# A hybrid attention and DeltaNet trunk: attention filled into the chunk scan by proportion, scores tied behind the scan's matmuls, output weights loaded from step 7

## The chip, the cores and the metric

The kernel runs on one core of a Trainium2 chip. The metric is the device time of one execution in microseconds (us); lower is better. The kernel before takes 2121.76 us, the median of three runs (2119.16 to 2123.61). The profiled execution took 2120.93 us. The engines are named as the profile names them: PE (TensorE matmuls), PEld (its weight loads), DVE (VectorE), ACT (ScalarE), POOL (GpSimd), SP (SyncE, which here only issues transfers).

## The reference, cut to what matters

Two layers run over 256 context tokens and 512 latent tokens of width 1024. In each layer one input projection feeds two kinds of heads that share one output projection; a mixture of experts follows.

```python
# softmax attention: 8 query heads, 2 key heads
s = einsum("bqkgd,bskd->bkgqs", q, k) * ATTN_SCALE
a = einsum("bkgqs,bskd->bqkgd", softmax(s), v)          # context rows attend in layer 0 only
# gated DeltaNet: 8 heads, chunks of 64 tokens, forward and backward
def step(state, xs):                                     # 12 chunks in order, one after another
    v_new = u_i - w_i @ state
    o_i   = qd_i @ state + a_i @ v_new
    state = state * exp(gl_i) + kd_i.T @ v_new
x = x + gate * (concat(a, norm(o) * silu(g)) @ w_out)    # output projection
x = x + gate2 * moe(modulate(norm(x)))                   # 32 experts, top 2
```

The modulation vectors (gates, shifts, scales) of the layer come from `silu(c) @ ada_w`, a matrix of 1024 by 6144 per layer. Attention and the scan need nothing of each other; the output projection needs both.

## The kernel before, in words

Every tile has 128 partitions. Matmul operands are split into a high and a low part, so a product takes three matmuls (`mm3`), and a score takes two (`attn_scores`, against the key stacks `ka` and `kb`).

The change lies in the part of `layer` that runs the scan and the attention together. It is run once per layer. Three streams are written as Python generators:

- **The scan**, `delta_step`, d: 12 steps, both directions at once. A step has four TensorE parts with VectorE or ScalarE work between them: `ks` (keys against the state; left out in step 0), `pz` (the chunk's corrected values, after DVE's `yt` and `lk`), `su` (the state's update, after DVE's `w`), then `po` and `pq` (the chunk's output, `pq` against the state; later added up by DVE in `ot` and by POOL in `o`). The generator yields eight times, after each TensorE part and after each part beside it.
- **The attention**, `attn_slots`, f: a unit is one query tile of one head. Four calls bring it on by scores (`sc`, into one PSUM buffer of two banks), maximum (DVE, `pp`), exponential and scale (ACT), transposes (`ptr`), high and low parts (`ph` by ACT, `pl` by DVE), values (`pv`) and output (`fu`, stored to `atd`). Layer 0 has 16 units of context and 32 of latent rows, layer 1 the 32.
- **The modulation**, `ada_steps`, a: `ada_w` is read in pieces of 1 MB (`araw`, two buffers, issued on POOL's queue) and multiplied (`aps`): 24 pieces in layer 0, 16 in layer 1.

In the kernel before, a string per step (`PAT`, three per layer, used in turn) says in which order the streams are called: one letter, one call. `step_load` brings the next step's chunk (`lk`, `lx`, `lq`) on SP's queue, and POOL multiplies `lq` into `lx`. From step 4 (`WS`) the first three quarters of `w_out` (`wr`, 1 MB each) are loaded on SP's queue too. Behind the loop they are split (`woh`, then `wol`, `m` or `wr` for the low parts), the fourth quarter is loaded into the first one's buffer, and the output projection (`po` of line 240) begins. Its tiles read the attention back (`al<-atd`) and turn the scan's output (`ot` of line 1048). Gates and shifts (`g`, `m`, `s`, with `h` for a norm's weight) come by broadcasting loads, which reuse the attention's memory.

The order in which the generators are called is not the order on the engines. A scheduler orders each engine's instructions by a simulation of its own; the calls give priorities, and a manual dependency without a semaphore (`add_manual_dep` with NoSync, or `issue_after`) fixes the order of two instructions of one engine. Each engine then runs strictly in that order: an instruction that waits holds up all that stand behind it on its engine or queue.

## Time and profile before

| | before |
|---|---|
| time, median of 3 runs | 2121.76 us |
| the profiled execution, its time and span | 2120.93 us, 2119.0 us |
| PE busy | 1768.4 us (83%) |
| DVE busy | 1459.2 us (69%) |
| ACT busy | 1019.6 us (48%) |
| POOL busy | 854.5 us (40%) |
| mean granted TensorE clock | 0.889 of full speed |
| loop of layer 0, first `pz` to last `pq` | 393.3 to 619.5 us |
| loop of layer 1, first `pz` to last `pq` | 1487.6 to 1655.9 us |

Busy time is an average over stages, so the profile is read by stretches. A stretch's length less PE's busy time is PE's idle time. The granted clock has two levels, 1.2 and 2.4 GHz; a value between them is a mean over the stretch, with 1.00 for 2.4 GHz. A wait stands in brackets behind the instruction that it delayed, with what ended it. The waits of an engine that is not late for anybody cost nothing.

### The profile page before, as it was taken

How to read it: one execution, taken by the hardware profiler on the slowest of the kernel's cores; microseconds unless marked ns; L12 is line 12 of the kernel's file. 1: busy time of each engine (PE TensorE's matmuls, PEld its weight loads, DVE VectorE, ACT ScalarE, POOL GpSimd, SP SyncE). 2: the span in 40 equal slices, each digit the busy share in tenths (PEclk: the TensorE clock that was granted, in tenths of full speed). 3: DMA queues.
4: the chain of work that ended last, by engine and by line, in shares of the span. 5: the costliest groups of instructions: out<-in, count | busy, mean ns of one | idle time of the engine just before them, and what ended most of it. 6: DMA issues, size and time to landing. Idle time of an engine off the chain costs nothing. (4 is left out here: it accounts for less than half of the span.)

```text
span 2119.0 us, 35656 instructions
## 1 busy us (share of the span) xinstructions
PE 1768.4 (83%) x13835; PEld 1388.6 (66%) x13835; DVE 1459.2 (69%) x2552; ACT 1019.6 (48%) x1595; POOL 854.5 (40%) x915
## 2 busy tenths in 40 slices
PE   6998898778976859998995987876898587999994
PEld 4887777655655747766764866765676475777773
DVE  4469996457772468987875579992587455787774
ACT  4444345445641136665554544333576224666663
POOL 4455653144354423233324466651233453334231
PEclk9998797679997979999997998975899698999997
DMA  8222436767655489998864223435983548988872
GB/s 279 78 82 77 119 112 176 232 191 212 209 135 124 116 310 334 331 333 322 312 223 122 75 73 93 137 108 162 273 241 104 143 179 326 344 335 327 334 296 98
DMA packets 227686, 427.80 MB, mean 202 GB/s; under 512 B 83720, under 2 KB 157180, under 8 KB 202939
## 3 DMA queue, kind: packets, MB, share of 16 engines
q1 hardware_dynamic: 171547, 329.09, 46.6%
q0 software_dynamic: 33536, 72.59, 12.0%
q10 hardware_dynamic: 22432, 23.81, 3.3%
q8 instruction: 110, 1.80, 0.4%
q14 instruction: 61, 0.50, 0.1%
HBM read 386.82 MB, written 84.67 MB: 223 GB/s over the span
## 5 line engine op out<-in xcount | busy, mean ns | idle before, releaser
L1421 POOL DMA_INDIRECT yd<-ey,idx x64 | 110.4, 1725 | 427.6 <-DMA yd<-ey,idx 120.8
L1367 PE MATMUL pab<-w,xt 128*128 128x512 f32 x512 | 230.3, 592 | 0.0
L1335 ACT ACTIVATE w2h<-w 128x2048 fp32r<-128x2048 f32 x64 | 122.7, 1917 | 130.9 <-PE py L1409 83.9
L1336 DVE TENSOR_TENSOR w2l<-w,w2h 128x2048 fp32r<-128x2048 f32 x64 | 147.8, 2309 | 45.8 <-ACT w2h L1335 45.8
L1336 DVE TENSOR_TENSOR w13l<-w,w13h 128x2048 fp32r<-128x2048 f32 x64 | 146.4, 2288 | 29.3 <-ACT w13h L1335 29.3
L1367 PEld LDWEIGHTS pab<-w,xt 128*128 128x128 f32 x512 | 93.0, 191 | 92.0 <-issue 91.8
L490 POOL TENSOR_TENSOR wlo<-wraw,whi 128x1024 fp32r<-128x1024 f32 (+1 forms) x44 | 113.6, 2586 | 92.5 <-ACT whi L489 92.5
L240 PE MATMUL pn<-whi,hh 128*128 128x256 f32 (+1 forms) x432 | 137.0, 320 | 12.9 <-ACT gev L1565 8.0
L240 PE MATMUL pn<-whi,hl 128*128 128x256 f32 (+1 forms) x432 | 135.7, 317 | 1.8 <-DVE hl L351 1.6
L240 PE MATMUL pn<-wlo,hh 128*128 128x256 f32 (+1 forms) x432 | 134.0, 311 | 1.2 <-POOL wlo L490 1.2
L240 PE MATMUL po<-woh,m 128*128 128x512 f32 x320 | 108.9, 419 | 24.6 <-ACT woh L1072 16.9
L1335 ACT ACTIVATE w13h<-w 128x2048 fp32r<-128x2048 f32 x64 | 121.7, 1902 | 6.3 <-DMA w<-w 3.9
L240 PE MATMUL pt<-hh,wlo 128*128 128x512 f32 (+1 forms) x352 | 123.5, 351 | 0.0
L240 PE MATMUL pt<-hh,whi 128*128 128x512 f32 (+1 forms) x352 | 122.1, 347 | 0.0
L240 PE MATMUL pt<-hl,whi 128*128 128x512 f32 (+1 forms) x352 | 121.5, 345 | 0.0
L1409 PE MATMUL py<-w2h,gh 128*128 128x512 f32 x256 | 108.8, 425 | 5.5 <-DVE ey L1416 4.4
L1416 DVE TENSOR_TENSOR ey<-py,eg 128x1024 f32<-128x1024 f32 x64 | 78.2, 1223 | 48.5 <-PE py L1409 36.2
L1340 POOL DMA_INDIRECT xe<-h2d,idx x64 | 87.0, 1359 | 60.8 <-issue 24.3
L519 DVE SCALAR_TENSOR_TENSOR dT<-xin,cw,dT 128x772 f32<-128x772 f32 x64 | 80.1, 1252 | 43.3 <-ACT dT L517 41.5
L1409 PE MATMUL py<-w2h,gl 128*128 128x512 f32 x256 | 102.7, 401 | 5.0 <-DVE gl L1388 5.0
L240 PEld LDWEIGHTS pn<-whi,hh 128*128 128x128 f32 x432 | 92.2, 214 | 19.3 <-ACT gev L1565 9.1
L1351 PEld LDWEIGHTS xt<-cst,xe 128*128 128x128 f32 x512 | 68.4, 192 | 55.3 <-issue 29.8
(402 smaller groups left out, 5130.4 us busy)
## 6 DMA issues: line engine op xcount, KB each, us to landing
w<-w SPq DMA_DIRECT2D x192, 1024.0 KB
araw<-ada_w POOLq DMA_DIRECT2D x40, 1024.0 KB, 8.6
wraw<-w_in SPq DMA_DIRECT2D x40, 512.0 KB
lk<-vk SPq DMA_DIRECT2D x48, 256.0 KB
lx<-xad SPq DMA_DIRECT2D x40, 256.0 KB
araw<-ada_w SPq DMA_DIRECT2D x8, 1024.0 KB
wr<-w_out SPq DMA_DIRECT2D x8, 1024.0 KB
vk<-vr ACTq DMA_DIRECT2D x16, 384.0 KB
```

Source lines behind the costliest of these rows:

```text
L240: self.nc.tensor.matmul(ps, a(k), b(k), start=(first and n == 0), stop=(last and n == 3 * nk - 1))
L490: getattr(nc, eng).tensor_tensor(lo, raw, hi, op=OP.subtract)
L519: nc.vector.scalar_tensor_tensor(dst, xin[:, tap:tap + 772], cw[:, tap, f:f + 1], dst, op0=OP.mult, op1=OP.add)
L1335: self.pin(nc.scalar.activation(hi, src, AF.Copy))
L1336: self.pin(nc.vector.tensor_tensor(lo, src, hi, op=OP.subtract))
L1340: self.pin(self.nc.gpsimd.indirect_dma_start(out=xe, out_offset=None, in_=h2d, in_offset=bass.IndirectOffsetOnAxis(ap=idx, axis=0), bounds ...
L1351: pin(nc.tensor.transpose(ps[:, k * P:(k + 1) * P], xe.rearrange("p (q k) -> p k q", k=8)[:, 4 * q + k, :], self.ident))
L1367: self.pin(self.nc.tensor.matmul(out, xt[:, k, :], w13[:, :, KS + k, :], start=False, stop=(k == 3)))
L1409: pin(self.nc.tensor.matmul(py[:, n * 512:(n + 1) * 512], a[:, j, :], b[:, c], start=(j + m == 0), stop=(j == 1 and m == 2)))
L1416: pin(nc.vector.tensor_tensor(y, py, gates, op=OP.mult))
L1421: self.pin(self.nc.gpsimd.indirect_dma_start(out=yd, out_offset=bass.IndirectOffsetOnAxis(ap=idx, axis=0), in_=y, in_offset=None, bounds_c ...
```

## The change

The strings `PAT` go. Behind each TensorE part of a step (every second yield) `advance` calls the attention and the modulation until both have had their share: all calls spread evenly over 11.5 of the 12 steps (`FS`), less the calls made ahead (`PRE`, 32 in layer 0, that is 8 units, and none in layer 1). Every score matmul is ordered behind the last matmul of the scan that was written in front of it (`step_mm`). The three loads of `w_out` are written from step 7 on instead of 4, one per step, and are ordered on SP's queue behind the load of `lx` that was written last (`stepx`).

```diff
-WS = 4
-PAT = (('fdfdfffdfffafddffffdfaffdfd', ...
+WS = 7
+PRE, FS = (32, 0), 11.5
...
     def attn_scores(self, u, st):
-                self.pin(self.nc.tensor.matmul(u.ps[:, a:b], qt, st[n][:, u.h // 4, a:b], start=(n == 0), stop=(n == 1)))
+                m = self.nc.tensor.matmul(u.ps[:, a:b], qt, st[n][:, u.h // 4, a:b], start=(n == 0), stop=(n == 1))
+                if self.step_mm is not None:
+                    self.tc.add_manual_dep(m.ins, self.step_mm, mybir.DependencyInfo(mybir.DependencyClass.NoSync, mybir.DependencyReason.DATA), reason="order")
...
     def step_load(...):
-            self.q("step").dma_start(x[rows[d], :np_], xad[tl[d], d, rows[d], :np_])
+            self.stepx = self.q("step").dma_start(x[rows[d], :np_], xad[tl[d], d, rows[d], :np_])
...
     def delta_step(...):        # so for ks, pq, pz, su and po
-                        pin(nc.tensor.matmul(ps[e][rows[d], ...
+                        self.step_mm = nc.tensor.matmul(ps[e][rows[d], ...).ins.name
...
     def layer(...):
             fill = self.attn_slots(work, st, qd, atd, pool)
+            total = dict(f=4 * (sum(2 * nq for _, _, nq, _ in work) + 2), a=4 * (4 if last else 6))
+            given = dict(f=0, a=0)
+            for _ in range(PRE[i]):
+                next(fill)
+                given["f"] += 1
+            ahead_f = PRE[i]
+
+            def advance(part):
+
+                for nm, gen, z in (("f", fill, ahead_f), ("a", ada, 0)):
+                    while given[nm] < z + part * (total[nm] - z):
+                        next(gen, None)
+                        given[nm] += 1
+
...
                 for s in range(12):
                     nkx = load(s + 1)
-                    step = self.delta_step(s, S, kx, dT, sc, o, seen, need(D0[s] // 2), p2)
-                    for c in PAT[i][s % 3]:
-                        next({"d": step, "f": fill, "a": ada}[c], None)
+                    for j, _ in enumerate(self.delta_step(s, S, kx, dT, sc, o, seen, need(D0[s] // 2), p2)):
+                        if j % 2 == 0:
+                            advance((4 * s + j // 2 + 1) / (4 * FS))
                     kx = nkx
                     if s >= WS and len(raws) < WP:
-                        raws.append(self.wout_raw(i, len(raws), wrp.tile([P, 2 * D], F32, name="wr", tag="wr%d" % len(raws))))
+                        with tc.issue_after(self.stepx.ins):
+                            raws.append(self.wout_raw(i, len(raws), wrp.tile([P, 2 * D], F32, name="wr", tag="wr%d" % len(raws))))
+                self.step_mm = None
```

Lines behind the edits move by 2 (helpers) to 18 (end of `layer`), so the same instruction has another line number in the rows of the change. No instruction is added or taken away: PE, DVE, ACT, POOL and SP have as many as before. The order is the same up to the end of layer 0's convolutions and in both expert stages.

SP's queue in layer 0's loop, before, where the first `w_out` loads stand (`lq`, `lk`, `lx`: the chunk of a step; `wr`: a quarter of `w_out`):

```order
L868 DMA lx<-xad_89 64x1024
L872 DMA lq<-qkd_90 64x512 x4
L1065 DMA wr<-w_out 128x2x1024 x3
L872 DMA lq<-qkd_90 64x512 x2
L867 DMA lk<-vk_88 64x1024 x2
L868 DMA lx<-xad_89 64x1024 x2
```

The same queue in the change, near the loop's end:

```order
L870 DMA lx<-xad_89 64x1024 x2
L1067 DMA wr<-w_out 128x2x1024
L874 DMA lq<-qkd_90 64x512 x2
L869 DMA lk<-vk_88 64x1024 x2
L870 DMA lx<-xad_89 64x1024 x2
L1067 DMA wr<-w_out 128x2x1024
L874 DMA lq<-qkd_90 64x512 x2
```

The three loads stood in one piece behind the chunks of the first two steps; they now stand one by one behind the chunks of steps 8, 9 and 10. In layer 1 they move in the same way. The fourth quarter moves forward a little: in layer 0 it stands behind the two gate loads `g` of line 1703 and two of the small `mm` loads, and in the change directly behind the four `m3t` loads; in layer 1 it stands behind two loads `al`, and in the change in front of them.

PE in layer 1, step 10 (one before the last), between values and state update, before:

```order
L648 MATMUL pv<-ph,vs 128x512
L648 MATMUL pv<-pl,vs 128x512
L920 MATMUL pz<-lk,lx 64x64 x16
L935 MATMUL su_16353<-w,lk 64x64
L935 MATMUL su_16354<-w,lk 64x64
```

The same place in the change:

```order
L605 MATMUL sc<-ka,qs 128x256
L605 MATMUL sc<-kb,qs 128x256
L266 MATMUL aps<-araw,scp 32x256 x8
L631 MATMUL ptr<-cst,pp 128x128 x6
L922 MATMUL pz<-lk,lx 64x64 x16
L605 MATMUL sc<-ka,qs 128x512
L605 MATMUL sc<-kb,qs 128x512
L605 MATMUL sc<-ka,qs 128x256
L605 MATMUL sc<-kb,qs 128x256
L937 MATMUL su_16411<-w,lk 64x64
L937 MATMUL su_16412<-w,lk 64x64
```

Before, the last values of the attention stand in front of this `pz`, and steps 10 and 11 have nothing beside them. In the change transposes and modulation stand in front of the `ks` of step 11 too, and the attention's last values between that `ks` and the last `pz` (in layer 0 behind the last `pz`).

DVE behind layer 1's loop, before (`yt`, `lk`: step 11; `s<-s,h`: a scale table for after the projection; `ot`: output of step 11; `m`, `wol`: operands of the output projection):

```order
L912 TENSOR_TENSOR yt_16496<-ks_16463,scs 128x4x64
L912 TENSOR_TENSOR yt_16496<-ks_16464,scs 128x4x64
L913 TENSOR_TENSOR lk<-lk,yt_16496 128x512
L1717 SCALAR_TENSOR_TENSOR s_16721<-s_16721,h_16792 128x1024
L959 TENSOR_TENSOR ot<-pq_16564,scs 128x4x64
L959 TENSOR_TENSOR ot<-pq_16565,scs 128x4x64
L960 TENSOR_TENSOR ot<-ot,po 128x512
L1051 TENSOR_TENSOR m_16592<-ot,m_16592 128x512
L1051 TENSOR_TENSOR m_16593<-ot,m_16592 128x512
L1073 TENSOR_TENSOR wol<-wr,woh 128x1024
```

The same place in the change:

```order
L962 TENSOR_TENSOR ot<-ot,po 128x512
L1053 TENSOR_TENSOR m_16623<-ot,m_16623 128x512
L1053 TENSOR_TENSOR m_16624<-ot,m_16623 128x512
L1075 TENSOR_TENSOR wol<-wr,woh 128x1024 x2
L1075 TENSOR_TENSOR m_16624<-wr,woh 128x1024
L1075 TENSOR_TENSOR wr<-wr,woh 128x1024
L1028 TENSOR_REDUCE oss<-o_16815 128x8
L1030 TENSOR_TENSOR oss<-oss,fq 128x8
L1031 TENSOR_TENSOR oss<-oss,fq 128x8
L1032 TENSOR_SCALAR oss<-oss 128x8
L1028 TENSOR_REDUCE oss<-o_16909 128x8
L1735 SCALAR_TENSOR_TENSOR s_16721<-s_16721,h_16792 128x1024
```

The scale table stood in front of the last output of the scan; it now stands behind it and behind the first four low parts of `w_out` that DVE makes. On ACT the six first `woh` stand in front of the second `m<-al` in layer 1 instead of behind it. In layer 0 the two last `wr<-wr,woh` of DVE stand in front of `sw<-mm,nmw` (line 308) instead of behind it.

## Rows read from the trace of the kernel before

**Rows 1.** Busy time by stretches: stretch, length, PE, PEld, DVE, ACT, POOL, clock, DMA, GB/s.

```profile
349.60:393.30 43.70, 37.98 (x363) 31.53 (x362) 20.34 (x69) 31.09 (x78) 3.35 (x5) 0.50 0.52 151
393.30:454.90 61.60, 37.99 (x523) 26.83 (x522) 24.95 (x66) 21.46 (x50) 19.07 (x23) 0.69 0.83 247
454.90:619.50 164.60, 139.03 (x2151) 106.60 (x2150) 120.43 (x279) 94.59 (x176) 69.38 (x75) 0.95 0.65 187
619.50:671.30 51.80, 27.35 (x102) 21.12 (x102) 23.58 (x28) 12.01 (x16) 20.45 (x13) 0.74 0.57 131
...
1487.60:1534.50 46.90, 39.76 (x497) 29.55 (x496) 28.44 (x67) 26.09 (x49) 11.47 (x14) 0.84 0.95 279
1534.50:1635.80 101.30, 93.77 (x1504) 72.90 (x1502) 84.51 (x194) 70.48 (x132) 33.20 (x38) 1.00 0.63 184
1635.80:1655.90 20.10, 10.74 (x257) 9.90 (x256) 8.88 (x22) 3.04 (x5) 13.06 (x13) 0.66 0.47 129
1655.90:1701.20 45.30, 24.62 (x101) 20.44 (x101) 21.41 (x27) 11.71 (x15) 19.76 (x12) 0.70 0.45 116
```

**Rows 2.** PE's waits from 393 to 455 us: total, times, longest.

```profile
PE aps L266 <- DMA araw<-ada_w: 16.6, 2, 13.7
PE sc L605 <- DVE qs L595: 5.3, 1, 5.3
```

**Rows 3.** Timeline of SP's queue, layer 0: start, duration, instruction.

```profile
398.16 1.61 SPq L1065 DMA_DIRECT2D wr<-w_out  x3
...
407.89 2.42 SPq L868 DMA_DIRECT2D lx<-xad  x2
```

**Rows 4.** Timeline of POOL, layer 0.

```profile
427.38 1.28 POOL L873 TENSOR_TENSOR lx<-lx,lq 128x512 f32<-128x512 f32 x1 [16.19 <-DMA lx<-xad]
...
440.97 0.74 POOL L232 DMA_DIRECT2D araw<-ada_w  x1
```

**Rows 5.** The tile `araw`: time from issue to landing.

```profile
DMA to landing us min/median/max: 5.2/8.6/16.8
```

**Rows 6.** PE's waits from 455 to 619.5 us.

```profile
PE aps L266 <- DMA araw<-ada_w: 9.0, 4, 3.8
```

**Rows 7.** Timeline of SP's queue, layer 1.

```profile
1493.39 1.10 SPq L1065 DMA_DIRECT2D wr<-w_out  x2
```

**Rows 8.** Timeline of PE, layer 1, early in the loop.

```profile
1515.21 1.30 PE L266 MATMUL aps<-araw,scp 128*32 128x256 f32 x16 [2.17 <-DMA araw<-ada_w]
1523.54 1.94 PE L266 MATMUL aps<-araw,scp 128*32 128x256 f32 x16 [3.61 <-DMA araw<-ada_w]
```

**Rows 9.** Timeline of PE, layer 1, the last steps and behind the loop.

```profile
1641.79 1.14 PE L935 MATMUL su<-w,lk 64*64 64x64 f32 x32 [4.82 <-DVE w L924]
...
1670.96 1.94 PE L1048 MATMUL ot<-cst,o 128*128 128x128 f32 x8 [15.10 <-DVE ot L959]
...
1681.78 1.65 PE L240 MATMUL po<-woh,m 128*128 128x512 f32 x3 [5.62 <-ACT woh L1072]
```

**Rows 10.** Timeline of DVE and ACT, behind layer 1's loop.

```profile
1669.25 1.23 DVE L1717 SCALAR_TENSOR_TENSOR s<-s,h 128x1024 f32<-128x1024 f32 x1 [19.15 <-DMA h<-norm_ffn_w]
...
1680.15 0.63 ACT L1044 ACTIVATE m<-al 128x512 fp32r<-128x512 f32 x1 [6.62 <-DMA al<-atd]
```

**Rows 11.** Timeline of PE, behind layer 0's loop.

```profile
657.52 1.22 PE L240 MATMUL po<-woh,m 128*128 128x512 f32 x2 [9.57 <-ACT woh L1072]
...
665.22 0.80 PE L240 MATMUL po<-wr,m 128*128 128x512 f32 x1 [5.30 <-DVE wr L1073]
```

**Rows 12.** Timeline of SP's queue, behind layer 0's loop.

```profile
630.76 7.73 SPq L1109 DMA_DIRECT2D m3t<-md  x4
...
644.57 0.89 SPq L1065 DMA_DIRECT2D wr<-w_out  x1
```

**Rows 13.** Timeline of ACT and DVE, behind layer 0's loop.

```profile
656.41 2.00 ACT L1072 ACTIVATE woh<-wr 128x1024 fp32r<-128x1024 f32 x2 [24.53 <-DMA wr<-w_out]
...
662.62 1.40 DVE L308 SCALAR_TENSOR_TENSOR sw<-mm,nmw 128x8 f32<-128x8 f32 x2 [16.32 <-DMA nmw<-norm_mix_w]
```

More of the change, by code (lines that the diff above doesn't have):

```diff
@@ L128 @@
 WP = 3
-WS = 4
-PAT = (('fdfdfffdfffafddffffdfaffdfd', 'fdfffdffdfdfafddffdfafffdfaf', 'fdffdfffdfdfafddffdfafffdff'), ('fdffdffadffdfddafdffdf', 'fdffdffadffdfddafdffdf', 'fdffdffddadffdfadd'))
+WS = 7
+PRE, FS = (32, 0), 11.5
 WB = 2
@@ L158, in __init__ @@
         self.pins(False)
-        self.seq = None
+        self.seq = self.step_mm = None
         self.mh = self.cp.tile([P, 32], F32, name="mh")
@@ L900, in by_state @@
                         r = slice(64 * e, 64 * e + 64)
-                        pin(nc.tensor.matmul(ps[e][rows[d], pr * HD:(pr + 1) * HD], dT[j][r, pr, col[d]:col[d] + 64], old[r, d, pr], start=True, stop=True, tile_position=(64 * e, half[d])))
+                        self.step_mm = nc.tensor.matmul(ps[e][rows[d], pr * HD:(pr + 1) * HD], dT[j][r, pr, col[d]:col[d] + 64], old[r, d, pr], start=True, stop=True, tile_position=(64 * e, half[d])).ins.name
             return [p[:, :256].rearrange("p (r i) -> p r i", r=4) for p in ps]
@@ L919, in delta_step @@
             for d in range(2):
-                pin(nc.tensor.matmul(pz[rows[d], h * HD:(h + 1) * HD], xa[rows[d], h], y[rows[d], h], start=True, stop=True, tile_position=(half[d], half[d])))
+                self.step_mm = nc.tensor.matmul(pz[rows[d], h * HD:(h + 1) * HD], xa[rows[d], h], y[rows[d], h], start=True, stop=True, tile_position=(half[d], half[d])).ins.name
         yield
@@ L934, in delta_step @@
                         e = a ^ d
-                        pin(nc.tensor.matmul(su[d][64 * e:64 * e + 64, pr * HD:(pr + 1) * HD], kn[rows[d], 2 * pr + e], w[rows[d], 2 * pr + e], start=True, stop=True, tile_position=(half[d], 64 * e)))
+                        self.step_mm = nc.tensor.matmul(su[d][64 * e:64 * e + 64, pr * HD:(pr + 1) * HD], kn[rows[d], 2 * pr + e], w[rows[d], 2 * pr + e], start=True, stop=True, tile_position=(half[d], 64 * e)).ins.name
         yield
@@ L950, in delta_step @@
                 for d in range(2):
-                    pin(nc.tensor.matmul(po[rows[d], h * HD:(h + 1) * HD], aa[rows[d], h], z[rows[d], h], start=True, stop=True, tile_position=(half[d], half[d])))
+                    self.step_mm = nc.tensor.matmul(po[rows[d], h * HD:(h + 1) * HD], aa[rows[d], h], z[rows[d], h], start=True, stop=True, tile_position=(half[d], half[d])).ins.name
             if s > 0:
```

## The prediction

> **What bounds the kernel now.** I read the busy time by stretches first, since the page's mean (PE 83%) mixes stages, then PE's waits in the stretches where it is idle, then the queue that each wait leads back to, and last the order of the change at those places. In both loops PE carries the work: from 1534.5 to 1635.8 us it is busy for 93.77 of 101.3 us at a clock of 1.00, and there is little to win [rows 1]. The time is lost around that. In layer 0, from 393.3 to 454.9 us, PE is busy for 37.99 of 61.6 us and has a clock of 0.69. In layer 1 the last two steps, 1635.8 to 1655.9 us, hold 10.74 us of PE work in 20.1 us, at 0.66. Behind the loops PE stands idle for 51.8 - 27.35 = 24.5 us and 45.3 - 24.62 = 20.7 us before the output projection runs freely [rows 1].
>
> What ends those waits is mostly a transfer. In the early stretch of layer 0, 16.6 us of PE's waiting are for `araw` and 5.3 us for `qs` [rows 2]. The chain behind the longest runs over two queues. SP issues 3 MB of `w_out` at 398.16 us and the chunk of a coming step only at 407.89 us [rows 3]. POOL waits 16.19 us for that chunk, and behind it in POOL's order, after a part of the next chunk, stands an `araw` that goes out at 440.97 us [rows 4]. PE, strictly in order, reaches `aps` with nothing loaded and waits for 13.7 us [rows 2]. The 5.3 us are DVE held up by the store of `atd`, which shares the same burst. Layer 1 has a smaller case: `wr` goes out at 1493.39 us [rows 7], and `aps` waits 2.17 and 3.61 us [rows 8].
>
> **The change part by part.** No instruction is added or removed, so every term is idle time or clock. The sum is made against the profiled execution, 2120.9 us, which is 0.8 us under the median.
>
> *Start of layer 0 (349.6 to 393.3).* Eight units are written ahead of the loop, and by the order nine stand in front of the first `pz`, where twelve did. PE is busy for 37.98 of 43.7 us at 0.50 there [rows 1], so three units of some 3 us at that clock leave this stretch and cost about 2/3 of it in the loop; one piece of `aps` moves the other way. I take 2 us, with bounds of -3 and 6, because the merges there are themselves a chain of PE and ACT.
>
> *Output weights later, layer 0.* With `w_out` gone from this place, the chunk no longer stands behind 3 MB, POOL comes to its `araw` sooner, and `atd` is stored in time. Of the 16.6 + 5.3 = 21.9 us I take 14 away. The rest stays, since the other 6 MB that the stretch moves (247 GB/s over 61.6 us is 15 MB in all) still come in bursts. With shorter waits the clock should rise: 37.99 us of work at 0.69 would take 31 us at 0.85; of these 7 us I take 4. Together 18, with bounds of 5 (only the waits for `qs`) and 27.
>
> The page "TensorE: Matmul & The Clock Gate" of the Trainium skill (section Part 1: The HAM clock gate) has it that sustained activity alone lifts the clock to 2.4 GHz. By that rule the whole stretch would go to full clock once the waits are gone, 37.99 x 0.31 = 12 us instead of 4, and the forecast would be 8 us lower. The start stretch speaks against counting on it: PE is busy there for 87% of the time and is granted 0.50 throughout [rows 1].
>
> *Output weights later, layer 1.* The waits of 2.17 and 3.61 us [rows 8] should go, and the clock of that stretch is 0.84 over 39.76 us of work [rows 1]. I take 5 and 3, so 8, bounds 0 and 12.
>
> *Where the weights go instead.* In each layer three loads of 1 MB now stand between the chunks of steps 8, 9 and 10. A piece of 1 MB takes 8.6 us from issue to landing [rows 5], and at the 279 GB/s of the densest stretch [rows 1] it occupies the DMA engines for 3.8 us. Six times 3.8 is 23 if every one is waited for. PE is seldom short of other work there, so I take -4, bounds 0 and -23. They stay early enough: their first reader is behind the loop.
>
> *Even fill, rest of layer 0 (454.9 to 619.5).* PE is idle for 164.6 - 139.03 = 25.6 us [rows 1], of which 9.0 us are waits for `araw` in four places [rows 6] and the rest waits of 0.2 to 3.3 us for DVE and ACT. One piece of modulation per two parts, where the strings had two close together, and about 0.9 unit of attention behind each part should take some of it. I take 6, bounds -8 and 14, since the new order can put waits where there are none.
>
> *Even fill, end of layer 1.* The strings use up the attention by 1635.8 us, and two steps run bare. At full clock their work is 10.74 x 0.66 = 7.1 us. With fill beside all but the last parts, some 4 us of bare waiting remain: 20.1 - 7.1 - 4 = 9 us saved, bounds 0 and 12.
>
> *Scores behind the scan's matmul.* Each score now waits where the scan's matmul in front of it waits. Queued behind it on PE are transposes and values of other units, on ACT and DVE the next exponential and maximum; the reader of all is a unit that is due a step later. The nearest row for a wait of that kind is the bare `su` with 4.82 us [rows 9], the other end is nothing. In the filled stretch of layer 1 PE idles for 7.5 us in about six steps [rows 1], waits of the same sort that fill does hide. I take that nearest row: half of it again over both layers, about -6, bounds 0 and -25.
>
> *Behind layer 1's loop.* PE waits 15.10 us at `ot` for a PSUM buffer that DVE must empty, and DVE sits 19.15 us in `s<-s,h` waiting for a load [rows 9, 10]. In the change that instruction stands behind the last `ot` and four low parts, so this wait goes. Then PE waits 5.62 us for `woh`, which ACT makes only after a second `al` that it waits 6.62 us for [rows 9, 10]; six `woh` now stand in front. What is late next: the attention ends some 6 us in front of the loop's end instead of 20, so its read-back `al` and the loads behind it on SP start later against that end; and the fourth quarter of `w_out` is waited for once the first three are used up, since it lands behind 4 to 5 MB of other loads. I leave 10 of the 20.7 idle us and give 1 to 2 us for the clock, so 12, bounds 4 and 16.
>
> *Behind layer 0's loop.* The second half of the idle time is the fourth quarter: it goes out at 644.57 us [rows 12], ACT waits 24.53 us for it, PE 9.57 us for ACT [rows 13, 11], and then DVE's low part stands behind `sw<-mm,nmw`, which waits 16.32 us for a load, so PE waits 5.30 us more [rows 13, 11]. In the change it goes out right behind `m3t`, whose issue ends at 638.5 us [rows 12], 6 us sooner, and DVE no longer has `sw` in front. If it lands 8.6 to 12 us later, the low part is there at about 653 instead of 665.2 us. Against that the attention ends 2 us later in respect to the loop's end. I take 10, bounds 0 and 16.
>
> Layer 1's convolutions are ordered a little differently too; without a place where one is better I count 0, bounds -4 and 4.
>
> **The sum.** 2 + 18 + 8 - 4 + 6 + 9 - 6 + 12 + 10 = 55 us. 2120.9 - 55 = 2066 us, 2.6% under before. Taking the half widths of the nine bounds (4.5, 11, 6, 11.5, 11, 6, 12, 6, 8) as independent spreads gives 27 us, and 1.28 times that, 34 us, either way for 8 in 10: 2032 to 2100.
>
> **The rivals.** *The burst is not what holds the early steps.* POOL waits in front of `araw` for PE's earlier `aps` as well, and the two buffers would leave the same holes with `w_out` elsewhere. For it: four waits for `araw` come long after the burst, 9.0 us [rows 6]. Against it: the longest two follow within 50 us of it and none later is over 3.8 us. The two terms of the weights, 18 and 8, are lost: 2066 + 26 = 2092 us.
>
> The page "DMA: Bandwidth & Descriptors" of the Trainium skill (section Rules for kernel authors) says to issue a transfer early and to wait for it late. By that rule the old place of `w_out` costs nothing, and the time is this rival's, 2092 us. The trace does not agree in this place: the chunk issued 10 us behind the burst holds POOL for 16.19 us [rows 4].
>
> *Gains of the tails given back.* The loads of the projection stage reuse the attention's memory. With the attention ending at the loop's end, PE may wait for `al` and the fourth quarter as long as it now waits for DVE. For it: in layer 0, where the attention already ends late, the idle time behind the loop is the larger one, 24.5 us. Against it: two of the waits there came from orders that the change turns round. The terms of 12 and 10 are lost: 2088 us.
>
> *Slower: the scan and its fill wait for each other.* With every score tied behind a scan matmul, a unit cannot run ahead while DVE and ACT (DVE busy for 120 of 165 us [rows 1]) are behind, and the next part finds no fill. The price is a bare wait in each step; the bare `su` shows 4.82 us, the two bare steps 20.1 - 10.74 = 9.4 us, so 4.7 us per step. The other terms save 61 us; over 24 steps the tie decides from 2.5 us per step on. At 3.5 us it is 84: 2121 - 61 + 84 = 2144 us. For it: one score buffer, so that a late maximum stops the next score. Against it: between `pz` and `su` the new order has scores or modulation in all but the last step.
>
> *It does not do what it says.* The scheduler had its own order before and has one now; if its view of the transfers is as wrong in the new places, the waits move only: 2121 us, give or take 4.
>
> **How the numbers follow.** Forecast 0.58, early steps not held by the burst 0.15, tails given back 0.12, slower 0.09, nothing 0.06. About 0.2% (4 us) can be told from no change here. Faster: the first three nearly whole, 0.84; the last is mostly within 0.2%, with edges of the others 0.06; slower 0.10. For 8 in 10 the range must hold the forecast's own 2032 to 2100 and the second and third case, 2088 and 2092 with 20 us of their own spread: 2032 to 2112 us.
>
> **What would show it.** Right: no wait of PE for `araw` over 5 us in layer 0, no wait of POOL for `lx` over 10 us before step 8, PE's `ot` behind layer 1's loop within 3 us of the last `pq`, and a stretch from first `pz` to last `pq` shorter by 20 to 30 us in layer 0 and by some 17 us in layer 1. Wrong: new waits at `pz`, `su` or `ks` for DVE of more than 2.5 us in most steps (the slower rival), waits for `araw` as long as before (the burst is innocent), or PE idle for over 20 us behind a loop again, now ended by `al` or `wr`.

## The result: 2097.98 us, a gain of 1.0% where 2.6% were forecast

The changed kernel takes 2097.98 us (median of 5 runs, 2092.01 to 2103.81), the kernel before 2119.16 us in the same comparison (5 runs). The ratio is 0.9898, 95% interval 0.9868 to 0.9928: 21.6 us saved where 55 were forecast. The time lies in the range of 2032 to 2112 us and the direction was right, but 21.6 is about 0.4 of 55. The profiled execution took 2092.01 us, the fastest of the five; a second one, profiled later (after_again), 2093.92 us.

PE's busy time rose from 1768.4 to 1777.3 us with the same 13835 matmuls; all that was saved is idle time of PE. The parts, each as length and in brackets PE's idle time (the sum of the gaps between its instructions), in us:

| part | before | after | after, second profile |
|---|---|---|---|
| layer 0, first score to first `pz` | 40.2 (4.5) | 40.2 (8.5) | 39.4 (9.2) |
| layer 0, loop, to last `pq` | 225.7 (48.7) | 216.5 (33.1) | 215.2 (29.2) |
| behind it, to last `po` | 126.8 (32.7) | 111.2 (16.4) | 111.2 (17.0) |
| layer 1, projection and convolutions, to first score | 329.9 (62.6) | 334.9 (62.0) | 337.0 (63.9) |
| layer 1, loop | 168.2 (24.0) | 163.7 (18.4) | 164.2 (19.0) |
| behind it, to last `po` | 79.0 (20.7) | 77.0 (18.4) | 76.7 (18.1) |

Together the parts are 26.3 us shorter in the first profile, of the 28.9 us by which the two profiled spans differ (2119.0 and 2090.1 us).

The stretches of the changed kernel that answer to [rows 1] (stretch, length, PE, PEld, DVE, ACT, POOL, clock, DMA, GB/s), cut at the same steps of the scan:

```profile
391.30:436.00 44.70, 33.93 (x492) 23.72 (x492) 20.77 (x60) 17.33 (x45) 17.37 (x21) 0.76 0.86 220
436.00:607.80 171.80, 149.42 (x2181) 111.85 (x2180) 124.38 (x294) 101.83 (x189) 68.18 (x72) 0.94 0.72 206
...
1464.70:1501.40 36.70, 33.86 (x451) 24.41 (x450) 26.11 (x60) 21.94 (x42) 9.35 (x11) 0.91 0.73 202
1501.40:1609.90 108.50, 97.11 (x1511) 74.18 (x1511) 84.70 (x192) 71.35 (x131) 37.64 (x42) 0.98 0.77 223
1609.90:1628.40 18.50, 14.25 (x300) 11.12 (x300) 14.25 (x35) 7.02 (x13) 11.31 (x12) 1.00 0.15 52
1628.40:1670.70 42.30, 23.96 (x94) 18.57 (x95) 21.40 (x26) 11.46 (x15) 19.91 (x12) 0.72 0.60 162
```

The early stretches are shorter by 61.6 - 44.7 = 16.9 and 46.9 - 36.7 = 10.2 us, about what was forecast for the later weights (18 and 8). But the stretches behind them are longer, by 7.2 us in layer 1 and 7.7 us in layer 0 (171.8 against the 164.1 us from 454.9 to the last `pq`). Part of what left the early stretch is work: PE has 492 matmul records there where it had 523.

PE's timeline in the changed kernel (start, duration, instruction, the wait in front of it with what ended it), at the first `pz` of layer 0 and behind layer 1's loop:

```profile
391.26 0.44 PE L922 MATMUL pz<-lk,lx 64*64 64x64 f32 x2 [5.96 <-DMA lx<-xad]
...
1628.96 1.06 PE L1050 MATMUL ot<-cst,o 128*128 128x128 f32 x8 [0.61 <-DVE ot L961]
1635.51 1.22 PE L240 MATMUL po<-woh,m 128*128 128x512 f32 x2 [5.49 <-ACT woh L1074]
1641.04 0.79 PE L240 MATMUL po<-wol,m 128*128 128x512 f32 x1 [4.31 <-DVE wol L1075]
...
1665.22 1.65 PE L240 MATMUL po<-woh,m 128*128 128x512 f32 x3 [6.73 <-ACT woh L1074]
```

The first row is a wait that the kernel before does not have. The wait of 15.10 us at `ot` [rows 9] is gone as forecast, 0.61 is left, but three waits for the split weights stand there now, where the kernel before had one, of 5.62 us [rows 9]. ACT's timeline at the same place shows why: the six splits `woh` stand behind the first `m<-al`, which waits for the attention's read-back.

```profile
1632.91 0.63 ACT L1046 ACTIVATE m<-al 128x512 fp32r<-128x512 f32 x1 [6.32 <-DMA al<-atd]
1633.45 1.06 ACT L1052 ACTIVATE m<-ot 128x512 fp32r<-128x512 f32 x2
1634.40 5.78 ACT L1074 ACTIVATE woh<-wr 128x1024 fp32r<-128x1024 f32 x6
...
1664.11 2.00 ACT L1074 ACTIVATE woh<-wr 128x1024 fp32r<-128x1024 f32 x2 [17.00 <-DMA wr<-w_out]
```

SP's queue behind the two loops:

```profile
615.80 7.04 SPq L1111 DMA_DIRECT2D m3t<-md  x4
622.93 0.97 SPq L1067 DMA_DIRECT2D wr<-w_out  x1
...
1643.21 6.94 SPq L1111 DMA_DIRECT2D m3t<-md  x4
...
1653.06 0.38 SPq L1067 DMA_DIRECT2D wr<-w_out  x1
```

In layer 0 the fourth quarter goes out 622.93 - 607.8 = 15.1 us behind the last `pq`, where it was 644.57 - 619.0 = 25.6 [rows 12], and PE's waits of 9.57 and 5.30 us [rows 11] are 2.23 and 1.36:

```profile
632.39 0.96 PE L240 MATMUL po<-woh,m 128*128 128x512 f32 x3 [2.23 <-ACT woh L1074]
634.73 0.58 PE L240 MATMUL po<-wr,m 128*128 128x512 f32 x1 [1.36 <-DVE wr L1075]
```

### The profile page after: what moved, and what is told of

Its sections match the earlier page's. It is cut to its first block, busy times and chain, and to the rows that moved or that the text cites. A ratio compares the mean times of both kernels' runs of the same rounds, so it can differ in the third digit from the quotient of the medians.

```text
span 2090.1 us, 35676 instructions
## 1 busy us (share of the span) xinstructions
PE 1777.3 (85%) x13835; PEld 1384.1 (66%) x13835; DVE 1460.8 (70%) x2552; ACT 1018.6 (49%) x1595; POOL 850.7 (41%) x915
## 5 line engine op out<-in xcount | busy, mean ns | idle before, releaser
L240 PE MATMUL pn<-whi,hh 128*128 128x256 f32 (+1 forms) x432 | 133.7, 313 | 12.5 <-ACT gev L1567 8.4
L240 PE MATMUL po<-woh,m 128*128 128x512 f32 x320 | 112.5, 431 | 24.4 <-ACT woh L1074 16.1
L1367 PE MATMUL pab<-w13h,xth 128*128 128x512 f32 x256 | 104.2, 407 | 0.5 <-ACT xth L1355 0.5
```

The costliest lines, as they stand in the source:

```text
L240: self.nc.tensor.matmul(ps, a(k), b(k), start=(first and n == 0), stop=(last and n == 3 * nk - 1))
L1367: self.pin(self.nc.tensor.matmul(out, a[:, k, :], b[:, :, k, :], start=(k + m == 0), stop=False))
```

## The experiments

### Which part brings the 21.6 us

**a_weights_only**: before, with `WS = 7` and `with tc.issue_after(self.stepx.ins):` around the load.

> The kernel before with one part of the change: the three loads of w_out from step 7 on, ordered behind the chunk's load. The fill keeps its strings, the scores are not tied. Theory (the prediction's, at half its size, since the loop of layer 0 shrank by 9 us and not by 20): the early burst is what the loop loses, so this part alone takes 9 us or more from first pz to last pq in layer 0 and 3 us in layer 1, the stretches behind the loops stay as before: about 2107 us against 2119. Rival (the burst is innocent, the waits for araw come from what stands in front of it on POOL): layer 0's loop stays within 4 us of its 225.7 us, waits for araw of over 10 us remain, the time is 2115 to 2121 us.

**b_weights_back**: changed, with `WS = 4` and without that line.

> The changed kernel with the w_out loads put back to step 4 and without their order behind the chunk; even fill and tied scores stay. Theory (burst): the loop of layer 0 grows by some 9 us to about 225 us and shows the waits for araw and the chunk behind the burst again: about 2108 to 2112 us. Rival (the even fill is what made the loop shorter): the loop stays within 4 us of 216.5 us and the time at 2096 to 2101 us.

**c_no_tie**: changed, with
```
-                if self.step_mm is not None:
+                if False:
```

> The changed kernel without the order of the scores behind the scan's matmuls. Theory (the prediction's term): the tie costs about 6 us, so 2092 us, with fewer waits at pz and ks. First rival: it costs nothing, 2095 to 2101 us. Second rival: the tie is what keeps the fill spread, and without it the scores bunch ahead of the loop, the last steps run bare again and the time is 2104 us or more.

**d_tie_only**: before, with `step_mm` and the manual dependency of the change.

> The kernel before with the scores tied to the scan's matmuls and nothing else. Theory (the prediction's term): the tie costs about 6 us, so 2125 us. First rival: nothing, 2115 to 2122 us. Second rival: the tie by itself orders the loop better and gives back part of the 21 us, 2112 us or less.

**n_fill_only**: c_no_tie and b_weights_back together.

> The even fill alone: the changed kernel without the tied scores and with the w_out loads from step 4 without an order. Theory (the parts depend on each other: the fill by itself gains nothing, it lets the later weights and the tied scores gain): 2118 to 2126 us, the loop of layer 1 as long as with strings. Rival (the prediction's terms, 6 us for the rest of layer 0's loop and 9 us for the last steps of layer 1, are there without the others): 2106 us or less.

| later weights | tied scores | even fill | median, us | ratio to before, 95% interval |
|---|---|---|---|---|
| yes | - | - | 2107.52 | 0.9937 (0.9914 to 0.9959) |
| - | yes | - | 2120.34 | 0.9995 (0.9980 to 1.0010) |
| - | - | yes | 2119.25 | 1.0002 (0.9988 to 1.0016) |
| - | yes | yes | 2113.82 | 0.9967 (0.9946 to 0.9988) |
| yes | - | yes | 2108.98 | 0.9943 (0.9922 to 0.9964) |
| yes | yes | yes | 2097.98 | 0.9898 (0.9868 to 0.9928) |

The later weights are worth 13.4 us alone (0.63% of 2121) and 14.6 in the changed kernel (0.9967 - 0.9898). The fill alone is worth nothing, the tie alone 1 us (neither can be told from no change), the two together 7, and the tie within the change 9.5 (0.9943 - 0.9898; the two intervals just touch). Beside the later weights alone the fill adds nothing either (0.9943 for 0.9937). The later weights with the tie and the old strings were not run, so whether the even fill is needed for the 21.6 us is not shown.

The theory on the weights holds in total, not in its parts. In a_weights_only layer 0's loop is 3.8 us shorter (221.9 for 225.7) where 9 were expected, by its length the rival's case; layer 1's is 3.3 us shorter, and 4.0 us come behind layer 0's loop, which was to stay as it was. With the weights back in their old place (b_weights_back) POOL waits 18.35 us for a chunk again, but PE's waits for `araw` in layer 0's loop are 3.4 us at most. That loop is 221.7 us for 216.5, and layer 1's 176.4 for 163.7, with a wait for `araw` of 8.04 us. n_fill_only's loop of layer 1 is shorter than with strings, against its theory (161.3 us, 18.9 idle, for 168.2 and 24.0); but its profiled execution, 2107.74 us, is the fastest of its twelve.

Where the weights act, in a_weights_only at the cuts of [rows 1]:

```profile
395.80:447.70 51.90, 35.81 (x522) 25.23 (x521) 24.60 (x65) 21.20 (x49) 18.33 (x22) 0.78 0.81 221
447.70:617.80 170.10, 145.24 (x2151) 110.66 (x2150) 119.99 (x278) 94.79 (x176) 69.99 (x75) 0.90 0.71 203
1480.10:1519.30 39.20, 36.78 (x499) 27.25 (x498) 28.41 (x67) 25.50 (x49) 11.43 (x14) 0.91 0.87 247
1519.30:1624.60 105.30, 94.00 (x1503) 73.90 (x1502) 84.04 (x194) 70.91 (x132) 33.34 (x38) 0.98 0.73 209
```

With the same records as before (522 for 523, 2151 for 2151) the early stretch of layer 0 is 9.7 us shorter: idle time 51.9 - 35.81 = 16.1 for 23.6, clock 0.78 for 0.69. The rest has the same idle time (24.9 for 25.1), but its clock is 0.90 for 0.95 and PE is busy 6.2 us longer. So the early rise of the clock was there, and no net gain of it remained. Over both loops, their starts and what follows them this kernel has 13 us less idle time, which is as much as its whole gain: 7.8 in layer 0's loop, 3.5 behind it, 1.0 in layer 1's loop.

The chain that was laid to the burst is halved, not gone. With no `w_out` in front, POOL still waits 9.05 us for a chunk (16.19 before [rows 4]) and PE 7.14 us for `araw` (13.7 before [rows 2]):

```profile
419.93 1.27 POOL L873 TENSOR_TENSOR lx<-lx,lq 128x512 f32<-128x512 f32 x1 [9.05 <-DMA lx<-xad]
```

On the tie the first rival holds where it stands alone. Where the fill is even, the time is the second rival's (2104 us or more). Its mechanism is there but small: without the tie the scores end 31 us in front of layer 1's last `pq` and not 16, and a `su` waits 5.97 us, yet PE's idle time in that loop is 19.7 us for 18.4.

Most of what the tie does lies behind layer 0's loop, where PE idles for 28.2 us without it (c_no_tie) and for 16.4 with it. In before, a_weights_only, c_no_tie and n_fill_only the fourth quarter goes out 22.5 to 25.6 us behind the last `pq`, with the tie (d_tie_only, b_weights_back, g_more_ahead below and the changed kernel's two profiles) 10.0 to 18.0. SP's queue and PE in c_no_tie, to be held against the rows above:

```profile
625.75 1.89 SPq L1721 DMA_DIRECT2D g<-md  x2
629.79 2.79 SPq L298 DMA_DIRECT2D mm<-md  x2
632.69 0.77 SPq L1067 DMA_DIRECT2D wr<-w_out  x1
```

```profile
646.53 1.22 PE L240 MATMUL po<-woh,m 128*128 128x512 f32 x2 [10.06 <-ACT woh L1074]
...
653.68 0.80 PE L240 MATMUL po<-wr,m 128*128 128x512 f32 x1 [4.75 <-DVE wr L1075]
```

These are the old waits. The order of SP there is the scheduler's, and the tie, which touches only scores, made it choose another one. Behind layer 1's loop c_no_tie is no better than before either: PE waits 20.01 us for `wol` there and idles for 22.7 us.

That the tie alone gains nothing hides two opposite effects. In d_tie_only PE idles less in layer 0's start and loop (41.6 us for 53.2) and behind that loop (20.2 for 32.7). But layer 1's loop idles for 28.9 us and not 24.0, PE is busy 13 us longer over the whole, and behind layer 1's loop nothing is won. The fourth quarter goes out 6.7 us behind the last `pq` and its split starts at 12.5 us, but the attention ends 5.3 us behind that `pq`, and PE waits for its read-back:

```profile
1667.45 0.79 PE L240 MATMUL po<-woh,m 128*128 128x512 f32 x1 [14.86 <-ACT m L1046]
...
1687.62 0.80 PE L240 MATMUL po<-woh,m 128*128 128x512 f32 x1 [6.17 <-ACT m L1046]
```

**after_again**: the changed kernel unaltered.

> The changed kernel unaltered, for the scatter of its parts. Kernels with the same order up to layer 1's tail differed by up to 9 us in layer 1's loop at nearly the same idle time of PE (18.0 and 19.2 us). Theory (lengths of a part scatter with the clock, idle time does not): idle time in both loops and behind them within 2 us of the first profile's 39.1, 16.4, 18.4 and 18.4 us. Rival (the waits scatter as well): over 4 us apart in one of them, and then no difference of that size between two single profiles counts.

By that count (39.1 contains the 6.0 us in front of the first `pz`) the idle times are 35.4, 17.0, 19.0 and 18.1 us: the first differs by 3.7, the others by under 1. In three of the four parts the theory holds; the first lies between theory and rival. So idle times of single profiles are good to some 4 us by these two, and lengths are worse: see l_gates_behind. A profile can also stand apart from its kernel's median (n_fill_only's by 11.5 us).

### Behind the loops

**e_split_first**: changed, with
```
-        nc.scalar.activation(mh[:, 0:4], a, AF.Copy)
+        am = nc.scalar.activation(mh[:, 0:4], a, AF.Copy)
+        if self.split3 is not None:          # the last woh of the first three quarters
+            self.tc.add_manual_dep(am.ins, self.split3, ...NoSync...)
```

> The changed kernel with one order added on ACT: the first m<-al behind each loop stands behind the six splits woh. In the changed kernel ACT waits 6.32 us for al behind layer 1's loop with the six splits, 5.78 us, queued behind it, and PE waits 5.5 and 4.3 us for them. Theory (the gain behind layer 1's loop was given back to this wait): the two waits shrink to 5 us together, layer 1's stretch from last pq to last po is 4 to 5 us shorter than 77.0 us, layer 0's about the same, 2093 us. Rival (the reused memory or DVE's parts hold the splits anyway): no change, 2096 to 2101 us.

2103.57 us, ratio 0.9926 (0.9904 to 0.9949): the theory fell, it is no gain. The splits run no earlier (ACT still starts with `m<-ot`), and `m<-al`, now last, is what PE waits for:

```profile
1644.02 0.79 PE L240 MATMUL po<-woh,m 128*128 128x512 f32 x1 [6.92 <-ACT m L1046]
1650.29 1.22 PE L240 MATMUL po<-woh,m 128*128 128x512 f32 x2 [4.20 <-POOL m L1050]
```

**f_split_and_quarter**: e_split_first, with `with tc.issue_after(wr3.ins):` around `logit_shift`, `wr3` being the fourth quarter's load.

> As e_split_first, and the four m3t loads stand behind the fourth quarter of w_out on SP's queue. In the changed kernel the quarter goes out at 1653.06 us in layer 1, behind m3t, whose issue takes 6.94 us, and PE waits 6.7 us for it, in layer 0 2.2 and 1.4 us. Theory: the quarter goes out 7 us or more sooner in layer 1, 4 us in layer 0, these waits go, 7 to 9 us less than e_split_first. Rival: the logits behind m3t (mb) become the wait in their place, within 3 us of e_split_first.

2116.50 us, ratio 0.9991 (0.9969 to 1.0013), slower than both expected. The loss lies behind layer 0's loop, where PE idles for 30.3 us and not 16.4. There SP's order came out otherwise: two `g` and the `mm` loads stand in front of the quarter, it goes out 17.9 us behind the last `pq` and not 15.1, and its split starts at 31.3 us and not 23.5. PE waits for it:

```profile
643.33 1.22 PE L240 MATMUL po<-woh,m 128*128 128x512 f32 x2 [7.38 <-ACT woh L1077]
651.70 0.79 PE L240 MATMUL po<-wr,m 128*128 128x512 f32 x1 [7.15 <-DVE wr L1080]
```

In layer 1 the quarter goes out 14.4 us behind the last `pq` and not 24.7, and its split starts at 34.4 us, where it was 35.8. SP's queue and ACT:

```profile
1658.95 2.17 SPq L1070 DMA_DIRECT2D wr<-w_out  x1
1661.23 9.66 SPq L1116 DMA_DIRECT2D m3t<-md  x4
```

```profile
1678.91 2.00 ACT L1077 ACTIVATE woh<-wr 128x1024 fp32r<-128x1024 f32 x2 [21.75 <-DMA wr<-w_out]
```

Issued 10 us sooner it lands at the same time. Between issue and split the DMA engines moved 3.8 MB here in 20 us, 2.3 MB in the changed kernel in 11 us, and 1.1 MB, hardly more than the quarter itself, in d_tie_only in 5.8 us. So it waits for other bytes; here 2.5 MB of them are loads of `g`, `m`, `h` and `wfin` that were issued in front of it and had not landed.

**g_more_ahead**: changed, with `PRE, FS = (44, 0), 11.5`.

> The changed kernel with 44 calls of the attention ahead of layer 0's loop for 32, so that twelve units' scores stand in front of the first pz, as before, and not nine. Theory (a cost of the tie that the prediction did not have: PE stands idle for 5.96 us at the first pz while the first chunk is written and read back, since the scores that used to fill it are tied behind that pz): the idle time at the first pz falls under 1 us, layer 0 from first score to last pq is 4 to 6 us shorter than 256.7 us, 2093 us. Rival (the units only move, and the loop's last steps lack them): within 3 us of 2098 us.

2092.01 us, ratio 0.9861 (0.9837 to 0.9885), as forecast, though the interval overlaps the changed kernel's (0.9868 to 0.9928). The wait at the first `pz` is gone, and from first score to last `pq` layer 0 takes 38.9 + 208.8 = 247.7 us for 256.7 (254.6 in the second profile):

```profile
396.92 0.44 PE L922 MATMUL pz<-lk,lx 64*64 64x64 f32 x2 [0.66 <-DMA lx<-xad]
```

**h_all_three**: f_split_and_quarter with `PRE` of 44.

> The three edits together: splits in front of m<-al, the quarter in front of m3t, 44 calls ahead. If each is a wait of its own, their sum, 16 to 19 us under the changed kernel: 2080 us. If the engines are at their limits in these stretches and the waits only change names, over 2092 us. The order of layer 1's projection is another one again, which alone has shown a difference of up to 6 us.

2104.54 us, ratio 0.9925 (0.9903 to 0.9946): the two edits behind the loops cost what they cost in f (PE idles for 32.3 and 23.8 us there, for 18.5 and 18.5 in g_more_ahead).

**l_gates_behind**: g_more_ahead, with `with tc.issue_after(wr3.ins):` around the loads of `g5` and `wfin`.

> The kernel with 44 calls ahead, and in each layer the loads of g5 and wfin (512 KB each, first read much later) behind the fourth quarter of w_out on SP's queue. The quarter landed 34.4 to 35.7 us behind layer 1's last pq wherever it was issued between 14.5 and 24.6 us behind it. Theory (it waits for the bytes that were issued in front of it): with 1 MB less in front it lands 4 us sooner in layer 1, PE's wait of 5.9 us for its split shrinks to 2, layer 0 as before: 2088 us. Rival (the small m3t loads in front hold the queue): it lands within 1.5 us of where it did, 2091 to 2093 us.

2086.75 us (5 runs), ratio 0.9851 (0.9830 to 0.9872), the lowest of all, but not to be told from g_more_ahead by its interval. The quarter goes out 21.6 us behind layer 1's last `pq`, and its split starts at 28.9 us for 36.0 in g_more_ahead, 7 us sooner for 3.7 us at the issue; behind that loop PE idles for 14.1 us for 18.5.

```profile
1664.85 0.39 SPq L1067 DMA_DIRECT2D wr<-w_out  x1
```

```profile
1672.13 2.00 ACT L1074 ACTIVATE woh<-wr 128x1024 fp32r<-128x1024 f32 x2 [10.84 <-DMA wr<-w_out]
```

**p_quarter_on_act**: g_more_ahead, with `(self.nc.scalar if u == 3 else self.nc.sync).dma_start(raw, ...)`.

> The kernel with 44 calls ahead, the fourth quarter issued on ACT's queue instead of SP's. Theory (order within one queue is what makes it late): it goes out some 13 us behind layer 1's last pq and lands at 28 us or sooner instead of 35, PE's waits for its split go (5.9 us in layer 1, 4.3 us in layer 0), in their place may come waits for s or g, which now share the engines: 2084 us. Rival (the engines' bandwidth is what makes it late, or ACT waits at the issue with m<-al behind it): 2091 us or more.

2093.21 us, ratio 0.9889 (0.9864 to 0.9914), the rival: the quarter goes out at 24.9 us, no sooner than on SP, since ACT stands at other work, and lands at 35.3.

**u_rows_behind**: l_gates_behind, with the first loads of `xs` ordered behind `wr3` too.

> As l_gates_behind, and the three loads xs (512 KB each) behind the fourth quarter too. Theory (what is issued in front of the quarter sets when it lands; with g5 and wfin behind it landed at 28.9 us behind the last pq and not at 36): with 1.5 MB less in front it lands at about 24 us in layer 1, PE's remaining wait of 3.4 us for it goes, 3 us less than l_gates_behind: 2084 us. Rival (the buffer of the first quarter, or the loads s and h, are the limit now, and xs becomes late for the norm): 2087 us or more.

2094.29 us, ratio 0.9873 (0.9839 to 0.9907), the rival: the split starts at 27.4 us for 28.9 and not at 24, so the bytes in front are not the only limit here, and behind layer 0's loop PE now waits 8.5 us for `ytm`, 26.6 us idle for 18.6.

### The waits for `araw`

**j_ada_on_act**: g_more_ahead, with `"scalar"` for `QUEUE["ada"]`.

> The kernel with 44 calls ahead, araw issued on ACT's queue instead of POOL's in both loops. With w_out later, PE still waits for araw: 2.4, 9.2, 2.8 and 2.1 us in layer 0's loop. Theory (POOL's order holds araw: POOL waits up to 11 us for the chunk lx in front of it): these waits fall under 4 us in sum, layer 0's loop is 8 us shorter. Rival (araw is late because its buffer comes free only when PE has used the piece before, or ACT then waits for that buffer with exponentials queued behind it): the waits stay or move to pp and ptr, the loop is not shorter, 2092 us or more.

2097.64 us, ratio 0.9908 (0.9889 to 0.9928), the rival. The waits for `araw` fall to 1.8 us, and others come (what waits for what: total, times, longest, layer 0's loop):

```profile
PE sc L605 <- DVE qs L595: 5.8, 1, 5.8
PE ptr L631 <- ACT pp L623: 4.4, 3, 3.5
...
PE aps L266 <- DMA araw<-ada_w: 1.8, 1, 1.8
```

**t_ada_late**: g_more_ahead, with `(part - 0.26) / 0.74` for the modulation's share in `advance`.

> The kernel with 44 calls ahead, the modulation's pieces spread over the last 74% of the steps and not over all, so that the 1 MB loads of araw stay out of the first three steps. Theory (traffic in the first steps is what PE still waits for there, 9.2 us for araw in the kernel with 44 calls ahead): PE's idle time in layer 0's loop, 30.3 us, falls by 6 us or more, the time to 2086 us or less. Rival (no wait for araw is a cost of its own; when it goes, DVE or ACT is late instead, as with araw on ACT's queue): idle time within 4 us, 2090 us or more.

2121.97 us, ratio 1.0002 (0.9986 to 1.0019): neither. In layer 0's loop the waits for `araw` are 20.8 us in six places for 16.9 in five, only later. In layer 1 the denser pieces meet the `w_out` loads, the loop takes 181.8 us with 33.7 idle, and the old chain is back: `w_out` goes out at 1603.07 us, `araw` at 1612.70 and 1614.75, a chunk at 1615.97, and POOL waits for it:

```profile
1628.18 1.26 POOL L875 TENSOR_TENSOR lx<-lx,lq 128x512 f32<-128x512 f32 x1 [11.58 <-DMA lx<-xad]
```

## Why the prediction was right in direction and wrong in size

The step that failed most is the even fill: the sum counted 15 us for it (6 and 9), and the runs show no time saved by it, neither alone (n_fill_only, ratio 1.0002) nor beside the later weights (0.9943 for 0.9937). Next come the end behind layer 1's loop (12 counted, 2 measured) and the weights in the loops (22 counted, 13 to 15 measured). That as much as 21.6 us remained is in part luck: the tie, counted as a cost of 6 us, gave back some 9.5 in the change, by an order of SP's queue behind layer 0's loop that the prediction used without knowing what made it.

- **Output weights later (18 and 8, less 4): right in part, 13 to 15 in size for 22.** In a_weights_only the waits for `araw` and `qs` in the early stretch fell as the chain of [rows 3, 4] has it, but from 21.9 to 14.2 us, 8 and not 14, since about half of the chain stands without `w_out`. Of the 15 MB that the stretch moves, the prediction set 6 against the 3 of `w_out`; there are 12, of which 6 are `araw`. In layer 1's loop 1.0 us of idle time went and not 5. The clock terms (4 and 3) did not come: what the early stretch won in clock the rest lost. Since kernels of one order differ as much in clock (below), no term of clock should have entered the sum. By the rule that was weighed there, to issue a transfer early (the Trainium skill, "DMA: Bandwidth & Descriptors", section Rules for kernel authors), this part would be worth nothing; a_weights_only's 13.4 us do not agree with it in this place. By the other, that sustained activity lifts the clock to 2.4 GHz (the Trainium skill, "TensorE: Matmul & The Clock Gate", section Part 1: The HAM clock gate), the early stretch would have been at 1.00; it is at 0.76 in the changed kernel, with a wait of 5.72 us left in it, so that the case which the rule speaks of did not arise.
- **Even fill (6 and 9): 0 alone, and 5 to 6 of idle time in layer 1.** The sum took the last two steps as 9 us saved. They are filled now: PE is busy for 14.25 of 18.5 us at clock 1.00, and the wait of 4.82 us is gone. But the fill comes out of steps in front of them, which are 7.2 us longer. Work that is moved between two stretches which PE's work fills nearly whole saves only the idle time that it fills there. That this is why the time gained nothing is argued from these stretches; no run separates it.
- **Start of layer 0 (2): 0.** The three units that left the start were the cover of the first chunk's write and read back; tied behind `pz` they can't run there. The prediction priced the tie at `su` and did not look at the first `pz`. The wait comes with the tie: it is 6.45 us in d_tie_only and 6.23 in b_weights_back, and c_no_tie and n_fill_only have none over 1.4 us there. g_more_ahead takes it away.
- **Tied scores (-6): +1 alone, +9.5 in the change.** PE's waits at `su` are 2.7 us over both loops where they were 5.6; the bare wait taken as the nearest row was the wrong one, since between the scan's parts there is now fill. Its arithmetic does not give the 6 either: 4.82 us and half of it again is 7.2.
- **Behind layer 0's loop (10): 15.6.** Mechanism as forecast, by the quarter's issue, which is some 10 us sooner where 6 were counted. That it hangs on the tie was not foreseen.
- **Behind layer 1's loop (12): 2.** The wait at `ot` went, as forecast. The "gains of the tails given back" rival is what happened here, though not in layer 0: ACT's splits (5.49 and 4.31 us) and the quarter (6.73) are late next. The six splits do stand in front of the second `m<-al`, as the prediction has it; but the attention ends only 3.5 us in front of the last `pq` (the prediction said 6), so now the first `m<-al` waits, 6.32 us, in front of them. The prediction named the quarter's 4 to 5 MB in front and still counted 12.
- **Layer 1's convolutions (0, bounds -4 and 4): -5.** In before and a_weights_only, whose order of PE is the same there, the part takes 329.9 us; in the 15 profiles with another order 332.6 to 341.0. The idle time is the same before and in the changed kernel (62.6 and 62.0 us), PE is busy longer. One group of it, before and in the changed kernel (ns minimum, median, maximum, first and last start), and each time the stretch that it fills, as in [rows 1]:

```profile
L781 PE MATMUL kk<-dT,dT x128: 218/218/267, 1348.1 to 1360.0; 64*64 64x64 f32 x128
...
1348.10:1360.30 12.20, 10.67 (x183) 9.65 (x183) 11.26 (x24) 6.79 (x15) 10.12 (x8) 1.00 0.41 109
```

```profile
L783 PE MATMUL kk<-dT,dT x128: 218/288/366, 1318.5 to 1341.5; 64*64 64x64 f32 x128
...
1318.50:1341.80 23.30, 16.30 (x184) 13.78 (x183) 22.36 (x54) 7.62 (x18) 14.49 (x10) 0.79 0.46 130
```

The same products stand together before, at a clock of 1.00, and are spread over twice the time in the changed kernel, with 7.0 us of waits among them and at 0.79: here the longer work is the clock. The nine profiles with exactly the changed kernel's order in this part take 333.8 to 337.6 us. That the order is the cause rests on this agreement; it was not forced back by itself.

The signs that the prediction gave: no wait for `araw` over 5 us in layer 0 (5.72 and 4.94 remain: missed by little), no wait of POOL for `lx` over 10 us before step 8 (10.92: missed by little), `ot` within 3 us (right), layer 0 shorter by 20 to 30 us and layer 1 by 17 (9.2 and 4.5: wrong), no waits of over 2.5 us at `pz`, `su` or `ks` for DVE in most steps (right: one, of 2.63 us). One of its readings was off: the second of the two early waits for `araw` is 2.9 us [rows 2], shorter than a later one of 3.8 [rows 6], so only the longest follows from the burst's place.

Still open is which of PE's waits for `araw` in layer 0 cost time: taking them away on ACT's queue saved 4 us of idle time in the loop and none of the time as a whole (2097.64 us for 2092.01).

## What to carry to other kernels

Add up idle time of the engine that bounds a loop over the whole loop, not lengths of its stretches: fill that moves shortens one stretch and lengthens another. Behind each wait that goes, write down what the same engine's queue holds next, with its own time; here the splits on ACT stood ready to take over. And where a scheduler sets the order, a local edit is also a change of order far away (+16 us behind one loop, -5 us in another layer): compare the orders there, too, before pricing the edit. A sum of savings needs each part tried with and without the others: here two parts that are worth nothing alone are worth 7 us together.

## What was not expected of the hardware

The clock differs between executions of one order. The five executions of l_gates_behind take 2082.41 to 2100.23 us, at mean granted clocks of 0.902 and 0.890. In layer 1's loop the profiled executions of l_gates_behind and g_more_ahead have the same order on PE and nearly the same idle time (18.0 and 19.2 us), in this order:

```profile
1472.20:1643.20 171.00, 152.99 (x2259) 115.95 (x2258) 125.56 (x284) 100.63 (x185) 57.31 (x64) 0.91 0.66 190
```

```profile
1468.10:1630.10 162.00, 142.81 (x2259) 108.25 (x2258) 125.92 (x284) 100.45 (x186) 57.68 (x64) 0.99 0.71 201
```

The loop takes 9 us longer with the same work, at a clock of 0.91 for 0.99. A single wait can be followed by such a fall: in a_weights_only PE waits 4.40 us for `araw` up to 558.46 us, and in the next 10 us it is busy throughout at 0.56, that is mostly at 1.2 GHz:

```profile
550.00:560.00 10.00, 4.87 (x63) 3.33 (x62) 6.15 (x12) 4.43 (x10) 2.90 (x3) 0.93 0.75 259
560.00:570.00 10.00, 10.00 (x112) 7.52 (x110) 2.81 (x8) 2.90 (x4) 3.08 (x4) 0.56 0.68 203
```
